# Planned times of DRAM round trips in a two-layer attention encoder

## The chip, the cores and the metric

The kernel runs on one core of a Trainium2 chip. The metric is the device time of one execution, in microseconds; less is better. Each time is the median of the runs made, and one further execution is taken with the hardware profiler, from which all the rows in this document come.

## What is computed

The input is 512 tokens of 1024 numbers, in float32. Two layers follow each other. Each has an RMS norm, one input projection, attention, a gate, an output projection and a residual sum. Layer A, with which the change deals, is dilated window attention with three groups of heads (dilation 1, 4 and 16), 16 heads of 64 in each:

```python
def mixer_a(hn, w_in, w_out, q_gain, k_gain, t5_bias):
    proj = hn @ w_in
    qkv = proj[..., :n_qkv].reshape(b, s, N_DIL_GROUPS, 3, N_HEADS, HEAD_DIM)
    gate = proj[..., n_qkv:]
    for g, (window, dilation) in enumerate(DILATED_PAIRS):
        q = rms_norm(qkv[:, :, g, 0], q_gain[g])
        k = rms_norm(qkv[:, :, g, 1], k_gain[g])
        v = qkv[:, :, g, 2]
        reach = (window // 2) // dilation
        o, lse = dilated_group_attention(q, k, v, t5_bias[g * N_HEADS:(g + 1) * N_HEADS],
                                         dilation, reach)
...
    alpha = jax.nn.softmax(jnp.stack(lses), axis=0)
    y = jnp.sum(alpha[..., None] * jnp.stack(outs), axis=0)
    y = y.reshape(b, s, BRANCH_WIDTH).astype(hn.dtype) * jax.nn.silu(gate)
    return y @ w_out
```

The merge over the three groups by their log denominators equals one softmax over the keys of all three groups together, and the kernel computes it so. Layer B is neighbourhood attention on a grid of 8 x 64 tokens.

## The kernel before

**Numbers and products.** Every float32 weight is split into a high and a low part of TensorE's fast float32 format (`split`, L128 to L139: ScalarE makes the high part `wh`, VectorE or POOL the low part `wl`). A product is then three matmuls: high times high, high times low, low times high (`mm3`, L221). Weights arrive in tiles `wraw` of 512 KB, three of which are in memory; four `wh` and four `wl` are. One split feeds 12 matmuls of 512 columns.

**Layer A by pairs.** The 16 heads are worked in 8 pairs, hc = 0 to 7. For each pair `main_a` projects the keys of two groups together with their values (`rawk`, 96 matmuls), the three groups' queries with the keys of the first (`rawq`, 96 matmuls), then the values of the first group (`v0_a`, 24) and the gate (`gate_a`, 24). The attention of pair hc does not run then. It runs while the next pair is projected: scores in two halves (u = 0 and 1, 96 short matmuls each), softmax, and the weighing of the values (`weigh`, 48 matmuls), which comes a further pair later, ahead of the next pair's scores.

**Trips through DRAM.** Queries and keys lie with tokens in the partitions after the projection, and the scores want heads there. In pairs 0 to 5 (`moved`, L458) the turn is not made on TensorE: VectorE scales the queries and keys by their norms (L313) and turns blocks of 32 x 32 (`turn_raw`, L525 to L530), one DMA writes all of it to DRAM (`qd`, 1536 KB, L654), and four DMAs read it back in the new order (`qt`, L660). Then ScalarE scales the keys (`split_q`, L675: first the keys `k`, L697, then two scalings in `qt`), and the scores can begin. Query buffer, key buffer and the raw queries exist once, so the write must be done before the next pair's keys come out of PSUM. The keys' part of the scaling is delayed (`normed`, L519 to L523), and the turn goes with it.

The first group's values take the same kind of trip (`move_v`, L567 to L589: written to `vd`, read back into `vt`, copied by ScalarE into `v0`), and so do the probabilities P (`turner`, L783: VectorE turns them into `tr`, one DMA writes 1024 KB to `td`, four of 256 KB read them into `pt`). The bias tables `e` are built in DRAM once and loaded for each pair by five DMAs (`bias_a`, L754 to L766).

**What sets the order.** TensorE's order is written by hand. `matmul` adds each matmul's planned time to a clock (`matmul`, L211 to L215), in nanoseconds of a plan and not of the chip. `later_on(delay, job)` emits a job when that clock has moved on by the delay, and the side work (attention) gives out waits such as `"wait", ("rawq", hc), 18000`: go on 18000 after the queries of this pair have been projected. So the constants of the plan say where in TensorE's order a DMA is issued or an operation emitted. The other engines' order comes from a scheduler that simulates the program; DMAs marked `keep_in_program_order` keep their order among themselves on SyncE's queue, which issues all transfers, and so do marked operations on VectorE and ScalarE. Whether an operation is late on the chip is decided by semaphores alone.

The planned times that are touched: the keys' scaling and turn (L520), the values' write, read and copy (L586 to L589), the step from projected queries to the move (L628), the read of the moved queries (L665), the second half's scores of pair 0 (L919), the read of P (L926), and the loading of the tables (L1202 to L1204). `land` (L667) lets the scaling of the moved keys be emitted as soon as the next pair's keys are projected; the first scores come 5200 behind that (L919).

Of the kernel before, what the change touches and what calls it, by code (L numbers as in the profile page):

```python
# [26 lines left out]
NHC = 8  # L27
# [19 lines left out]
def tile_hybrid_encoder(  # L47
# [187 lines left out]
    def later_on(delay, job):  # L235

        timers.append((clock[0] + delay, job))
        timers.sort(key=lambda t: t[0])
# [57 lines left out]
    def head_norm(raw, ss, ns, held, delay=0, quick=False, then=None):  # L296


        rs = wk.tile([P, 32], F32, tag="rs", name="rs")
        rsqrt(nc.vector if ns == 8 or quick else nc.gpsimd, rs[:, : 4 * ns], ss[:, : 4 * ns], 4 * ns, 1.0 / DH)  # L300

        def scale():
            for i in range(4):
                by = rs[:, i * ns : (i + 1) * ns].unsqueeze(2)
                if isinstance(raw, str):
                    f0, f1 = FS[raw]
                    v = by_block[:, :, i, :].rearrange("p (h a f) r -> p f h a r", h=2, f=6)[:, f0:f1]
                    by = rs[:, i * ns : (i + 1) * ns].rearrange("p (f h) -> p f h", h=2)
                    by = by.unsqueeze(3).unsqueeze(4).to_broadcast([P, f1 - f0, 2, 2, 32])
                else:  # L310
                    v = raw[:, i, : ns * 64].rearrange("p (a b) -> p a b", b=64)
                    by = by.to_broadcast([P, ns, 64])
                m = nc.vector.tensor_mul(v, v, by)  # L313
                if held or delay:
                    tc.keep_in_program_order(m)
            if then:
                then()

        if held:
            later.append(scale)  # L320
        elif delay:
            later_on(delay, scale)
        else:
            scale()
# [121 lines left out]
    st = {}  # L446
    pq = wk.tile([P, 4096], F32, tag="pt", name="pt", bufs=1)
# [10 lines left out]
    moved = lambda hc: hc < NHC - 2  # L458
# [58 lines left out]
        normed(raw, ss, ns, key, hc)  # L517

    def normed(raw, ss, ns, key, hc):  # L519
        delay = (31000 if moved(hc) else 9000) if key == "rawk" and 0 < hc < NHC - 1 else 0  # L520
        head_norm(raw, ss, ns, False, delay, then=partial(turn_raw, key) if moved(hc) else None)
        st[key, hc] = raw
        stamp[key, hc] = clock[0]  # L523
# [43 lines left out]
    def move_v(hc, vt):  # L567

        d = dr.tile([4, P, P], F32, name="vd", tag="vd", bufs=2)
        vx = wk.tile([P, 4, 4, 32], F32, tag="vx", name="vx", bufs=1)  # L570
        nc.vector.transpose(vx.rearrange("p b i r -> p i b r"), vt.rearrange("p (i b r) -> p i b r", i=4, b=4))

        def write():
            tc.keep_in_program_order(nc.sync.dma_start(d.rearrange("b p x -> p b x"), vx.rearrange("p b i r -> p b (i r)")))

        def read(b):
            dst = vt[32 * b : 32 * b + 32].rearrange("k (a x) -> k a x", a=4)
            tc.keep_in_program_order(nc.sync.dma_start(dst, d[b].rearrange("(a k) x -> k a x", a=4)))

        def place():  # L580
            src = vt.rearrange("p (a i r) -> p i a r", a=4, i=4)
            dst = v0[hc % 2].rearrange("p i (a r) -> p i a r", a=4)
            tc.keep_in_program_order(nc.scalar.copy(dst, src))
            stamp["v", hc] = 0

        later_on(2500, write)  # L586
        for b in (0, 2, 1, 3):
            later_on(7000, partial(read, b))
        later_on(12500, place)  # L589

    def main_a(hc):
        parts = (
# [32 lines left out]

    def q_a(hc):

        yield "wait", ("rawq", hc), 18000 if moved(hc) else 13000 if hc < NHC - 1 else 23500  # L628
        raw = st.pop(("rawq", hc))
        if moved(hc):  # L630
            move_q(hc)
            return
        qt, k0 = q_tiles(hc)

        tp = transpose4(raw, 0)
        nc.scalar.copy(qt[:, :, 0, :].rearrange("p t (j r) -> p t j r", j=4), to_tjr(tp))
        yield
        tp = transpose4(raw, 3 * P)
        scaled(trj(k0[:, 64:EXT]), to_trj(tp), 0)
        yield  # L640
        for g in range(2):
            tp = transpose4(raw, (g + 1) * P)
            nc.vector.tensor_copy(qt[:, :, 1 + g, :].rearrange("p t (j r) -> p t j r", j=4), to_tjr(tp))
            yield
        stamp["q", hc] = 0

    def move_q(hc):

        d = dr.tile([4, P, 768], F32, name="qd", tag="qd", bufs=2)
        qt, k0 = q_tiles(hc)  # L650
        left = [4]

        def write():
            tc.keep_in_program_order(nc.sync.dma_start(d.rearrange("a p x -> p a x"), by_a))  # L654
            stamp["q", hc] = 0

        def read(a):
            dst = qt[32 * a : 32 * a + 32].rearrange("k t f x -> k t (f x)")
            src = d[a].rearrange("(t k) x -> k t x", t=4)
            tc.keep_in_program_order(nc.sync.dma_start(dst, src))  # L660
            left[0] -= 1

        later_on(600, write)
        for a in (0, 2, 1, 3):
            later_on(5500, partial(read, a))  # L665

        def land():  # L667
            yield "wait", ("rawk", hc + 1), 0
            assert not left[0]
            split_q(qt, k0)  # L670
            yield

        st["land", hc] = land()
# [80 lines left out]
    def bias_a(hc):  # L754
        e0 = wk.tile([P, 2, 256], F32, tag="e0", name="e0")
        e12 = wk.tile([P, 4, 224], F32, tag="e12", name="e12")
        hs = slice(2 * hc, 2 * hc + 2)

        def load(dst, src):
            tc.keep_in_program_order(nc.sync.dma_start(dst, src))  # L760

        load(e0, l0_d[hs].rearrange("h p c -> p h c"))
        for j in range(4):
            dst = e12[32 * j : 32 * j + 32].rearrange("p (h g) c -> p h (g c)", h=2)
            load(dst, l12_d[hs].rearrange("h r c -> r h c"))
        return e0, e12  # L766
# [46 lines left out]
    def attn_a(hc):  # L813
# [99 lines left out]
        if hc < NHC - 1:  # L913
            for u in range(2):
                if moved(hc):
                    if pending and u == 0:
                        pending.pop(0)()
                        yield
                    yield "wait", ("rawk", hc + 1), 5200 if u == 0 else 16800 if hc else 14200  # L919
                else:  # L920
                    yield 6500 if u == 0 else 7000
                turned = turner(512)
                turners.append(turned)
                for hd, t, pr in scores(u):
                    turned.put(pr, 512, 256 * hd + 128 * (t % 2))
                send = partial(turned.send, pq[:, 2048 * u : 2048 * u + 2048], 8500, 1200)  # L926
                later_on(7000 + 2000 * u, send)
                if pending and u == 0:
                    yield 5000
                    pending.pop(0)()  # L930
            pending.append(lambda: put_y(hc, weigh(), True, False))
        else:
            for u in range(2):
                if u == 0:
                    yield "wait", ("gate", hc), 500
                yield 600
                held = scores(u)
                yield 3200
                if pending:
                    yield "wait", ("gate", hc - 1), 16800  # L940
                    pending.pop(0)()
                    yield
                for args in held:
                    turn_p(*args)
                    yield
            yield from v_a(hc)
            stamp["ya", "turned"] = 0
            put_y(hc, weigh(), True, True)
            yield
# [248 lines left out]

    def main():
        for hc in range(NHC):  # L1200
            if hc == 1:
                later_on(20000, lambda: st.__setitem__(("e", 1), bias_a(1)))  # L1202
            elif hc:
                st["e", hc] = bias_a(hc)  # L1204
            yield from main_a(hc)
        yield from out_product("ya", sink_a)
        gap[0] = cycle((500, 500, 800))
        for hc in range(2):
            st["e", hc] = bias_b(hc)
        for kind, i in B_PARTS:  # L1210
            if kind == "qk":
                yield from project_qk(512, 4, "raw", i, ("qk", 2 * i - 1) if i else ("rs", "b"))
            elif kind == "v":
                yield from project_qk(512, 0, "v", i, None)
            else:
                yield from gate_b(i)
        yield from out_product("yb", sink_b, True)
# [153 lines left out]
```

## Time and profile before

| what | us |
|---|---|
| median of 3 runs | 846.79 |
| the runs | 4705.28, 846.79, 845.79 |
| the profiled execution | 845.74 |
| its span, first to last instruction | 844.0 |
| TensorE busy | 831.6 |
| VectorE busy | 516.2 |
| ScalarE busy | 430.4 |
| POOL busy | 282.2 |

The mean granted TensorE clock of the profiled execution is 0.995 of full speed, and the DMA engines moved 154.08 MB at a mean of 183 GB/s. TensorE's busy time counts a matmul from its start to a modelled end, and neighbours overlap, so a busy TensorE says only that no gap is seen, and the sum over groups is more than the span. For the pace one looks at how many matmuls a stretch holds.

In the rows of the timeline the columns are: start in us from the span's start, duration in us, engine, line, operation, what it writes and reads, form, number, and in brackets how long the engine stood idle before it and what ended that. In the rows of waits they are: total us, times, longest us. A window's row has, per engine, busy us and instructions, then the granted clock, the share of the 16 DMA engines, and GB/s. In the chain a row is start, us, what.

### The profile page before, as it was taken

The page shows a single profiled execution, that of the slowest core. Times are in us where ns is not written, and L with a number is a line of the kernel's source. Part 1 is how long each engine was busy: PE and PEld are TensorE (multiplying, and loading weights), DVE is VectorE, ACT ScalarE, POOL GpSimd, SP SyncE. Part 2 cuts the span into 40 slices and gives each one's busy share as a digit, 9 for nine tenths or more (in the row PEclk, how much of TensorE's full clock was granted, in tenths as well). Part 3 has the DMA queues.
Part 4 walks back from the last instruction along what each step waited for, and adds up shares of the span by engine and source line. Part 5 has one row for each costly group of instructions (what it writes and reads, how often), then busy time and mean ns, then how long its engine had stood idle before and what let it go on. Part 6 is the DMA issues. An engine that isn't in the chain of part 4 may idle for free.

```text
span 844.0 us, 15462 instructions
## 1 busy us (share of the span) xinstructions
PE 831.6 (99%) x5616; PEld 669.3 (79%) x5616; DVE 516.2 (61%) x1356; ACT 430.4 (51%) x905; POOL 282.2 (33%) x424
## 2 busy tenths in 40 slices
PE   9999999899999999999999999999999999999998
PEld 7888777688788688788788788888878877777787
DVE  7374575476576467467475665538565678668653
ACT  7443653553653652652662564435366466673551
POOL 2261442442432441441431341112431625225211
PEclk9999999999999999999999999999999999999999
DMA  6487679569569569669668464265226546447323
GB/s 252 131 238 233 179 213 276 169 206 288 164 207 283 134 185 290 181 188 290 182 201 233 139 181 107 67 216 181 100 93 179 167 150 178 136 146 211 103 93 132
DMA packets 73324, 154.08 MB, mean 183 GB/s; under 512 B 6640, under 2 KB 32368, under 8 KB 73248
## 3 DMA queue, kind: packets, MB, share of 16 engines
q1 hardware_dynamic: 73104, 152.83, 60.4%
q8 instruction: 44, 0.72, 0.4%
q10 hardware_dynamic: 144, 0.26, 0.1%
q14 instruction: 32, 0.26, 0.1%
HBM read 117.04 MB, written 39.04 MB: 185 GB/s over the span
## 4 chain that ended last, share of the span: by engine, by line
PE 72%; DMA 13%; DVE 7%; ACT 4%; issue 2%; SPq 1%; POOL 1%; ACTq 0%; DVEq 0%; POOLq 0%
PE acc L215 62%; DMA qt<-qd 5%; PE log L215 4%; DMA qd<-rawq 4%; PE o L215 3%; PE tp L219 2%; DMA e<-l_d 2%; DVE rawq L313 2%; DVE rawq L530 1%; DVE wl L138 1%; ACT p L1140 1%; DMA wraw<-in_w 1%; ACT p L724 1%; ACT qt L697 1%; DMA td<-tr 1%
## 5 line engine op out<-in xcount | busy, mean ns | idle before, releaser
L215 PE MATMUL acc<-wh,hn_h 128*128 128x512 f32 x704 | 281.9, 401 | 1.5 <-ACT hn_h L404 0.6
L132 ACT CAST wh<-wraw 128x512 fp32r<-128x512 f32 (+1 forms) x259 | 157.7, 612 | 235.1 <-PE acc L215 215.1
L215 PE MATMUL acc<-wl,hn_h 128*128 128x512 f32 x704 | 275.0, 391 | 0.2 <-DVE wl L138 0.2
L215 PE MATMUL acc<-wh,hn_l 128*128 128x512 f32 x704 | 274.6, 391 | 0.0
L138 POOL TENSOR_TENSOR wl<-wraw,wh 128x512 fp32r<-128x512 f32 (+1 forms) x104 | 136.4, 1312 | 388.8 <-ACT wh L132 348.3
L138 DVE TENSOR_TENSOR wl<-wraw,wh 128x512 fp32r<-128x512 f32 (+1 forms) x156 | 112.7, 723 | 140.7 <-ACT wh L132 140.2
L215 PEld LDWEIGHTS acc<-wh,hn_h 128*128 128x128 f32 x704 | 132.7, 189 | 38.1 <-issue 6.0
L215 PEld LDWEIGHTS acc<-wh,hn_l 128*128 128x128 f32 x704 | 133.0, 189 | 28.6
L215 PEld LDWEIGHTS acc<-wl,hn_h 128*128 128x128 f32 x704 | 133.2, 189 | 26.2 <-DVE wl L138 0.5
L215 PE MATMUL acc<-y,wh 128*128 128x512 f32 (+1 forms) x272 | 82.4, 387 | 0.0
L215 PE MATMUL acc<-hn_h,wh 128*128 128x512 f32 x192 | 76.1, 396 | 1.2 <-ACT rawk L493 0.6
L215 PE MATMUL acc<-hn_h,wl 128*128 128x512 f32 x192 | 74.8, 390 | 0.0
L215 PE MATMUL acc<-hn_l,wh 128*128 128x512 f32 x192 | 74.8, 389 | 0.0
L724 ACT ACTIVATE p<-p,mn 128x512 f32<-128x512 f32 (+3 forms) x128 | 69.6, 585 | 1.1 <-DVE mn L723 0.7
L290 DVE TENSOR_REDUCE ss<-sq 128x4 f32<-128x256 f32 (+1 forms) x96 | 48.4, 505 | 32.6 <-POOL sq L287 22.5
L878 ACT ACTIVATE p<-p,mn 128x512 f32<-128x512 f32 (+1 forms) x64 | 44.8, 702 | 35.1 <-DVE mn L867 34.7
L794 DVE STREAM_TRANSPOSE tr<-p 128x512 f32<-128x512 f32 (+1 forms) x80 | 53.8, 685 | 12.4 <-ACT p L724 10.0
L313 DVE TENSOR_TENSOR rawq<-rawq,rs 128x256 f32<-128x256 f32 (+1 forms) x96 | 55.0, 632 | 4.1 <-POOL rs L124 3.7
L215 PEld LDWEIGHTS acc<-y,wh 128*128 128x128 f32 x272 | 48.3, 189 | 9.6 <-issue 1.3
L215 PE MATMUL acc<-y,wl 128*128 128x512 f32 (+1 forms) x136 | 51.4, 378 | 0.0
L287 POOL TENSOR_TENSOR sq<-rawq 128x256 f32<-128x256 f32 (+1 forms) x48 | 42.6, 900 | 17.6 <-ACT rawq L493 15.9
L493 ACT ACTIVATE rawq<-acc,rs_n 128x512 f32<-128x512 f32 (+1 forms) x76 | 44.9, 611 | 2.8 <-DMA qd<-rawq 2.5
(123 smaller groups left out, 941.1 us busy)
## 6 DMA issues: line engine op xcount, KB each, us to landing
wraw<-in_w SPq DMA_DIRECT2D x119, 512.0 KB
td<-tr SPq DMA_DIRECT2D x14, 1024.0 KB
pt<-td SPq DMA_DIRECT2D x56, 256.0 KB
qd<-rawq SPq DMA_DIRECT2D x6, 1536.0 KB
qt<-qd SPq DMA_DIRECT2D x24, 384.0 KB
td<-tr SPq DMA_DIRECT2D x6, 896.0 KB
pt<-td SPq DMA_DIRECT2D x24, 224.0 KB
e<-l_d SPq DMA_DIRECT2D x32, 112.0 KB
```

The lines of the kernel that those rows point to most:

```text
L132: nc.scalar.copy(h, raw)
L138: eng.tensor_sub(l, raw, h.bitcast(F32))
L215: nc.tensor.matmul(o, l, r, **kw)
L219: nc.tensor.transpose(o, i, ident)
L287: nc.gpsimd.tensor_mul(sq.rearrange("p (f a r) -> p a f r", a=4, r=32), v, v)
L290: nc.vector.tensor_reduce(ss[:, i * ns : (i + 1) * ns], sq.rearrange("p (a b) -> p a b", b=64), axis=AX.X, op=ALU.add)
L313: m = nc.vector.tensor_mul(v, v, by)
L493: nc.scalar.activation(dst, src, AF.Copy, scale=rs_n[:, i : i + 1])
L530: tc.keep_in_program_order(nc.vector.transpose(x, x))
L724: nc.scalar.activation(pr, pr, AF.Copy, scale=mn[:, 3:4])
L794: nc.vector.transpose(dst, src[:, :n].rearrange("p (i b k) -> p i b k", b=4, k=32))
L878: nc.scalar.activation(row, row, AF.Exp, bias=mn[:, 1:2], scale=-1.0, accum_out=mn[:, 2:3])
```

## The change

Constants of the plan change, and the loading of the tables gets one form for all pairs. No computation, transfer or buffer is added or taken away.

- Pairs 0 to 5: the queries' move begins 8000 behind their projection and no longer 18000; its reads stand 6500 and no longer 5500 behind the move's begin.
- The keys' scaling and turn: 11000 behind their projection (pair 1: 22000) and no longer 31000.
- The values' write, read and copy: 26000, 32000 and 38000 behind their projection (pair 6: 8000, 13000, 18500) and no longer 2500, 7000 and 12500.
- The tables of each pair from 1 on: 26000 after the pair's begin; before, pair 1 had 20000 and the others 0.
- P's second half: its reads begin 6000 behind its write, 500 apart, and no longer 8500 and 1200 apart.
- Pair 0's second half of scores: 12500 and no longer 14200 behind the next pair's keys.

```diff
@@ normed @@
-        delay = (31000 if moved(hc) else 9000) if key == "rawk" and 0 < hc < NHC - 1 else 0
+        delay = ((22000 if hc == 1 else 11000) if moved(hc) else 9000) if key == "rawk" and 0 < hc < NHC - 1 else 0
@@ move_v @@
-        later_on(2500, write)
+        out, back, there = (26000, 32000, 38000) if moved(hc) else (8000, 13000, 18500)
+        later_on(out, write)
         for b in (0, 2, 1, 3):
-            later_on(7000, partial(read, b))
-        later_on(12500, place)
+            later_on(back, partial(read, b))
+        later_on(there, place)
@@ q_a @@
-        yield "wait", ("rawq", hc), 18000 if moved(hc) else 13000 if hc < NHC - 1 else 23500
+        yield "wait", ("rawq", hc), 8000 if moved(hc) else 13000 if hc < NHC - 1 else 23500
@@ move_q @@
         later_on(600, write)
         for a in (0, 2, 1, 3):
-            later_on(5500, partial(read, a))
+            later_on(6500, partial(read, a))
@@ attn_a @@
-                    yield "wait", ("rawk", hc + 1), 5200 if u == 0 else 16800 if hc else 14200
+                    yield "wait", ("rawk", hc + 1), 5200 if u == 0 else 16800 if hc else 12500
...
-                send = partial(turned.send, pq[:, 2048 * u : 2048 * u + 2048], 8500, 1200)
+                send = partial(turned.send, pq[:, 2048 * u : 2048 * u + 2048], *((6000, 500) if u else (8500, 1200)))
@@ main @@
-            if hc == 1:
-                later_on(20000, lambda: st.__setitem__(("e", 1), bias_a(1)))
-            elif hc:
-                st["e", hc] = bias_a(hc)
+            if hc:
+                later_on(26000, lambda hc=hc: st.__setitem__(("e", hc), bias_a(hc)))
```

## The prediction

> **What bounds the kernel now.** I read the page first, then TensorE's waits, its timeline where they fall, the chain, and last the other engines around one stage. The head and part 1 of the page:
>
> ```profile
> span 844.0 us, 15462 instructions
> ...
> PE 831.6 (99%) x5616; PEld 669.3 (79%) x5616; DVE 516.2 (61%) x1356; ACT 430.4 (51%) x905; POOL 282.2 (33%) x424
> ```
>
> TensorE is drawn busy for all but 12.4 us. No edit here removes a matmul, so only idle time and matmuls that run slower than their like can go. TensorE's waits say where the idle time is (total us, times, longest):
>
> ```profile
> PE log L215 <- ACT k L697: 4.5, 4, 2.0
> PE acc L215 <- ACT rawk L493: 1.0, 2, 0.6
> ...
> PE acc L215 <- DVE wl L138: 0.2, 1, 0.2
> ```
>
> The largest is the change's subject: the first scores of a head pair wait for ScalarE's scaling of the moved keys. Here is the start of that score block for pairs 0 to 5, from TensorE's timeline (start, us):
>
> ```profile
> 91.92 0.56 PE L215 MATMUL log<-k,qt 64*32 64x192 f32 x16
> 155.83 0.50 PE L215 MATMUL log<-k,qt 64*32 64x192 f32 x8 [1.98 <-ACT k L697]
> 220.47 0.51 PE L215 MATMUL log<-k,qt 64*32 64x192 f32 x9
> 285.65 0.66 PE L215 MATMUL log<-k,qt 64*32 64x192 f32 x16 [1.81 <-ACT k L697]
> 350.53 0.50 PE L215 MATMUL log<-k,qt 64*32 64x192 f32 x8 [0.25 <-ACT k L697]
> 414.27 0.51 PE L215 MATMUL log<-k,qt 64*32 64x192 f32 x9 [0.50 <-ACT k L697]
> ```
>
> And the projection run behind each block, from the chain in order of time (its start is the block's end):
>
> ```profile
> 93.89 7.07 PE acc L215 x31
> ...
> 159.44 10.16 PE acc L215 x42
> ...
> 223.06 9.74 PE acc L215 x42
> ...
> 289.26 10.13 PE acc L215 x42
> ...
> 353.12 9.77 PE acc L215 x42
> ...
> 416.86 9.74 PE acc L215 x42
> ```
>
> Pair 0, which waits for nothing, takes 93.89 - 91.92 = 1.97 us for its 96 score matmuls. Pairs 1 and 3, after waits near 2 us, take 3.61; pairs 2, 4 and 5 take 2.59. So a late key costs three things: the wait, a longer block (the second and third scaling are late as well), and after a long wait a lower clock, which the stage rows show (us, busy by engine, granted clock, DMA share, GB/s):
>
> ```profile
> 155.80:159.40 3.60, 3.41 (x97) 2.02 (x97) 1.45 (x8) 3.21 (x5) 1.81 (x2) 0.66 0.09 31
> ...
> 192.00:202.00 10.00, 10.00 (x46) 8.29 (x45) 9.51 (x19) 3.22 (x6) 1.33 (x1) 1.00 1.09 261
> 202.00:210.00 8.00, 8.00 (x37) 6.64 (x36) 1.38 (x2) 1.97 (x4) 2.57 (x2) 1.00 1.03 366
> ...
> 219.00:230.00 11.00, 10.82 (x133) 8.16 (x133) 7.14 (x26) 10.22 (x19) 3.65 (x5) 1.00 0.19 70
> ```
>
> What makes the keys late is the trip of queries and keys through DRAM. Pair 1's in the chain, then ScalarE's rows for the scaling in pairs 0, 1 and 3:
>
> ```profile
> 137.04 8.20 DMA qd<-rawq
> 146.61 7.89 DMA qt<-qd
> ```
>
> ```profile
> 90.00 1.24 ACT L697 ACTIVATE k<-qt,gk 128x512 f32<-128x512 f32 x1 [2.60 <-DMA qt<-qd]
> ...
> 154.60 1.17 ACT L697 ACTIVATE k<-qt,gk 128x512 f32<-128x512 f32 x1 [5.75 <-DMA qt<-qd]
> ...
> 284.42 1.17 ACT L697 ACTIVATE k<-qt,gk 128x512 f32<-128x512 f32 x1 [5.58 <-DMA qt<-qd]
> ```
>
> In pair 0 the scaling starts 91.92 - 90.00 = 1.92 us ahead of the scores, and nothing is lost. TensorE alone would have reached pair 1's block at 155.83 - 1.98 = 153.85 and pair 3's at 283.84. So the keys need to be 154.60 - (153.85 - 1.92) = 2.7 us sooner in pair 1, 2.5 us in pair 3, and less in the others. That is the amount that decides.
>
> **The change, part by part.**
>
> *Write sooner (L628: 18000 to 8000), scale of the keys sooner (L520: 31000 to 11000, pair 1 to 22000).* The delays count on the kernel's own clock, which adds up matmul times. Before, write and turn came out together; pair 2's VectorE, POOL and SP rows:
>
> ```profile
> 184.38 2.26 DVE L313 TENSOR_TENSOR rawq<-rawq,rs 128x256 f32<-128x256 f32 x4
> 186.56 0.67 DVE L290 TENSOR_REDUCE ss<-sq 128x8 f32<-128x512 f32 x1
> ...
> 187.82 1.29 DVE L530 STREAM_TRANSPOSE rawq<-rawq 128x512 f32<-128x512 f32 x2
> ...
> 198.78 2.36 DVE L530 STREAM_TRANSPOSE rawq<-rawq 128x1024 f32<-128x1024 f32 x2
> ```
>
> ```profile
> 183.87 1.49 POOL L287 TENSOR_TENSOR sq<-rawq 128x512 f32<-128x512 f32 x1
> ```
>
> ```profile
> 202.18 0.43 SPq L654 DMA_DIRECT2D qd<-rawq  x1
> ...
> 209.90 1.74 SPq L660 DMA_DIRECT2D qt<-qd  x4
> ```
>
> The queries' turn ends at 201.14 and the write goes out at 202.18. An earlier planned write alone therefore buys only about 1 us: the data is not ready. The keys' scale (2.26) and turn (1.29) are in front of it on VectorE. With them gone, the last square sum can follow POOL's square, done at 185.36, and not wait until 186.56 (1.2 us); the keys' turn saves 1.29 more. So the turn ends 2.5 us sooner, and the write goes out at about 198.7, 3.5 us sooner. The bounds are 1.0 (only the gap behind the turn) and 1.04 + 2.26 + 1.29 = 4.6; I take 3.5, which stands on single rows.
>
> The 3.55 us of VectorE work does not vanish. It moves into the first softmax (pair 1's behind the second), in a stretch where VectorE is busy 7.14 of 11 us: 3.9 us are free, so it fits, but just. If that cover is gone, P's turn and its write come up to 3.55 us later; the scores of the second half need only the logits' banks.
>
> *Read back (L665, 5500 to 6500).* From the write's plan the reads stand 5.9 instead of 4.9 us. They wait for the write to land anyway (209.90 is 7.7 us behind 202.18), so this costs nothing while the write takes over 5.9 us. The four reads, in SP's order, still hold up weight loads behind them.
>
> *Values' write, read and copy (L586 to L589) and bias tables (L1202, L1204) later.* Per pair this shifts one write of 256 KB, four reads of 64 KB, five table loads (704 KB, from the tiles' shapes) and one ScalarE copy. Today they run ahead of the query write, at 192 to 202, where the DMA engines are full (share 1.09). Together 1216 KB: at 261 GB/s, 4.8 us of traffic that no longer stands in front of the queries. They move to where the share is 0.19 (219 to 230). Nobody waits for them there: tables are due at the pair's own scores, a pair later, values at its weighing, later still. Pair 6, which moves no queries, has the same in small (5.5 to 6 later). Bounds for the queries' landing: 0, if the weights take the room, to 4.8. I count none of it beside the 3.5; it is my margin over the needed 2.7.
>
> The price is on ScalarE: the copy waits there for the values' reads, and weight splits stand behind it. Before:
>
> ```profile
> 138.45 0.62 ACT L583 COPY v<-vt 128x512 f32<-128x512 f32 x1 [8.83 <-DMA vt<-vd]
> ```
>
> That wait of 8.83 us cost TensorE only the 0.2 us of the wl row above, and the 5.75 us wait at 154.60 cost it no split at all. So a wait below 5.75 us is free and one of 8.83 nearly so. At the new place ScalarE is busy 10.22 of 11 us; a wait there delays softmax too. Bounds: a gain of 0.2 (the wait at 138 goes) to a loss of 8.83 x 6 = 53 us if nothing covered it; I take 0.5 of loss, near the row that cost 0.2.
>
> *P's second half read back sooner (L926: 8500, 1200 to 6000, 500).* Four reads of 256 KB go before the query write instead of between its parts. SP stands still if P's write has not landed:
>
> ```profile
> SPq L807 <- DMA td<-tr: 27.6, 10, 5.8
> ```
>
> One such wait is at most 5.8 us today and starves nothing; I take 0.5 in all, bounds 0 to 5.8. *Pair 0's second scores (L919, 14200 to 12500)* come 1.7 us sooner on the clock. Their matmuls are the same and softmax of the first half covers them: 0; without that cover its P buffer, a single one, would hold VectorE, not TensorE.
>
> **The sum.** Waits: 1.98 + 1.81 + 0.25 + 0.50 = 4.54. A matmul is drawn 0.39 long, but 42 take 9.74 us, 0.23 each, so every one of the four waits is really 0.16 longer: 0.64. Longer blocks: 2 x (3.61 - 1.97) + 3 x (2.59 - 1.97) = 5.14. Slower runs behind pairs 1 and 3: 0.42 + 0.39 = 0.81. One row more goes with the sooner write, which held the evacuation of the next keys:
>
> ```profile
> 146.22 0.50 PE L215 MATMUL acc<-wh,hn_h 128*128 128x512 f32 x1 [0.34 <-ACT rawk L493]
> ```
>
> That is 0.34. All together 11.5 gained, 1.0 given back: 10.5 less. The profiled execution took 845.74 us (span 844.0), so 835.2; the median of the runs, 846.79, stands 1.05 above it, so 836.3.
>
> A page's rule weighs against part of this. The Trainium skill, "TensorE: Matmul & The Clock Gate", Part 1, states that the array's clock falls to half after an idle window of about 3.4 us. By that a 2 us wait should cost no clock, and the slow blocks would have another cause and stay. The trace disagrees: 0.66 granted behind 1.98 us of idling, 1.00 in the row that holds pair 2.
>
> **The rivals.**
> *A, forecast, 836.3:* keys 2.7 us sooner or more in all pairs.
> *B, partly:* VectorE or full DMA engines leave only 1.5 us. Then pairs 2, 4, 5 lose nothing (0.75 + 0.32 + 1.86 gained) and pairs 1 and 3 gain 3.0 of wait but keep 2.59 long blocks (2.04 + 0.81 gained): 8.8 - 1.0, so 839.0; with 0.5 us sooner, some 843. For it: share 1.03 to 1.09 at that place. Against: 1.2 MB less in front.
> *C, slower:* the values' copy stops ScalarE inside softmax. It decides once the wait passes 8.8 us, behind which each further us is TensorE's. With 12 us in each of six pairs, 6 x 3.2 = 19 us lost against 10.5 won: 855. Under 10.5 us each it is no slower than before. For it: this wait reached 8.83; the tables load beside it now. Against: 960 KB of reads at 261 GB/s are 3.8 us, in a stretch with a share of 0.19.
> *D, the clock loss is not the wait's:* the part of pairs 1 and 3 above the other blocks (2 x 1.02 + 0.81 = 2.85) stays: 839.2.
> *E, no effect:* write and reads stay tied to the same landing: 846.8.
>
> **How the numbers follow.** Chances: A 0.66, B 0.14, C 0.08, D 0.06, E 0.06. The time is A's: 836.3. A's own range is 832 to 840: 832 if no price is paid and the 4.8 us also ease later waits, 840 if the prices reach 5. Range for 8 in 10: 831.5 to 844.5, which takes in A, B and D and leaves C and E out. About 2% is what a measurement tells from no change here: that is under 829.9 or over 863.7. Faster by more would take 17 us, beyond the 12.4 us idle plus what slow blocks hold: 0.03. Slower needs C with over 27 us lost: 0.04. Same: 0.93.
>
> **What would show it.** Right: the k row gone from TensorE's waits or under 1 us; blocks of 1.97 us in all six pairs; query writes at least 2.5 us sooner in their stage; no clock under 0.9 between pairs. The keys' scale should lie behind the first softmax. Wrong: ScalarE's values' copy with waits over 8.8 us and TensorE waiting on wh or wl; the wait at log named for logits' banks or P; SP's rows for wraw late behind P's reads.

## The result, and the profile after

The changed kernel takes 830.5 us (median of 4 runs, 830.22 to 832.05). The four runs of the kernel before that belong to this comparison took 4705.28, 846.79, 845.79 and 843.77 us (median 846.29); the ratio leaves the first of them out. The ratio is 0.9827, with a 95% interval of 0.98 to 0.9854: 1.7% faster, some 14.6 us, which is less than the 2% that the prediction takes as the mark of a change. Forecast were 836.3 and a range from 831.5 to 844.5. As measured, the time lies 1.0 us below the range; the ratio applied to the 846.79 from which the prediction counted gives 832.1, which is just inside. The profiled execution took 830.22 us.

The head, TensorE's share and the chain's shares by engine on the page of the changed kernel, and behind them the chain's shares before:

```profile
span 828.4 us, 15450 instructions
...
PE 822.4 (99%) x5616; PEld 667.2 (81%) x5616; DVE 509.5 (62%) x1356; ACT 431.5 (52%) x905; POOL 281.7 (34%) x424
...
PE 94%; ACT 2%; DVE 2%; issue 0%; DMA 0%; DVEq 0%; ACTq 0%
```

```profile
PE 72%; DMA 13%; DVE 7%; ACT 4%; issue 2%; SPq 1%; POOL 1%; ACTq 0%; DVEq 0%; POOLq 0%
```

TensorE's share of the chain that ended last has gone from 72% to 94%, DMA's from 13% to 0%. All of TensorE's waits that the view lists:

```profile
PE busy L379 <- DVE warm L368: 0.9, 1, 0.9
PE acc L215 <- ACT rawk L493: 0.6, 1, 0.6
PE acc L215 <- ACT hn_h L404: 0.6, 1, 0.6
PE acc L215 <- ACT rawq L493: 0.5, 2, 0.3
PE acc L215 <- DVE pt L1039: 0.2, 1, 0.2
```

The row for the scaled keys, 4.5 us before, is gone, and so is the one of `qt` (0.8 us). The first scores of pairs 0 to 5, from TensorE's timeline:

```profile
89.79 0.56 PE L215 MATMUL log<-k,qt 64*32 64x192 f32 x16
...
149.54 0.56 PE L215 MATMUL log<-k,qt 64*32 64x192 f32 x16
...
211.98 0.54 PE L215 MATMUL log<-k,qt 64*32 64x192 f32 x13
...
274.45 0.56 PE L215 MATMUL log<-k,qt 64*32 64x192 f32 x16
...
336.93 0.56 PE L215 MATMUL log<-k,qt 64*32 64x192 f32 x16
...
399.41 0.56 PE L215 MATMUL log<-k,qt 64*32 64x192 f32 x16
```

None has a bracket: no wait. From pair 1 on they stand 62.5 us apart; before it was 63.7 to 65.2. The chain shows the block of pair 1 undivided and the run behind it at the quick pace:

```profile
149.61 1.84 PE log L215 x96
151.46 9.74 PE acc L215 x42
```

Where did the time go? Pair 0 to pair 5 took 414.27 - 91.92 = 322.35 us and takes 399.41 - 89.79 = 309.62: 12.7 less. From there to the end it was 429.7 and is 429.0. The remaining 2.1 us lie ahead of pair 0, where the change touches nothing yet; the last section shows that they are a matter of the start. So the two profiled executions differ by 15.5 us, of which 13.5 can be the change's.

The move of pair 2, from ScalarE's evacuation of the queries over VectorE's turn to SyncE's queue; first before:

```profile
178.78 2.51 ACT L493 ACTIVATE rawq<-acc,rs_n 128x512 f32<-128x512 f32 x4
```

and after:

```profile
170.38 2.51 ACT L493 ACTIVATE rawq<-acc,rs_n 128x512 f32<-128x512 f32 x4
```

```profile
186.51 2.36 DVE L530 STREAM_TRANSPOSE rawq<-rawq 128x1024 f32<-128x1024 f32 x2
```

```profile
186.05 0.35 SPq L184 DMA_DIRECT2D wraw<-in_w  x1
188.90 0.38 SPq L655 DMA_DIRECT2D qd<-rawq  x1
190.18 0.34 SPq L184 DMA_DIRECT2D wraw<-in_w  x1
196.56 1.74 SPq L661 DMA_DIRECT2D qt<-qd  x4
198.41 3.35 SPq L184 DMA_DIRECT2D wraw<-in_w  x2
201.82 0.43 SPq L574 DMA_DIRECT2D vd<-vx  x1
202.30 3.60 SPq L761 DMA_DIRECT2D e<-l_d  x5
```

The write was 23.4 us behind the start of the evacuation (202.18 - 178.78) and is 18.5 us behind it (188.90 - 170.38): 4.9 us sooner. The same subtraction gives 4.8 to 4.9 us in pairs 3 to 5, and 3.2 in pair 1. It leaves when the turn ends, at 188.87. Nothing but weights stands beside the trip; values and tables come behind the reads.

### The profile page after: what moved, and what is told of

Its sections match the earlier page's. It is cut to its first block, busy times and chain, and to the rows that moved or that the text cites. A ratio compares the mean times of both kernels' runs of the same rounds, so it can differ in the third digit from the quotient of the medians.

```text
span 828.4 us, 15450 instructions
## 1 busy us (share of the span) xinstructions
PE 822.4 (99%) x5616; PEld 667.2 (81%) x5616; DVE 509.5 (62%) x1356; ACT 431.5 (52%) x905; POOL 281.7 (34%) x424
## 4 chain that ended last, share of the span: by engine, by line
PE 94%; ACT 2%; DVE 2%; issue 0%; DMA 0%; DVEq 0%; ACTq 0%
PE acc L215 82%; PE o L215 5%; PE log L215 5%; PE tp L219 2%; ACT p L1141 1%; ACT p L725 1%; DVE hn_l L405 1%; DMA x_all<-in_xt 0%; DVE rawq L313 0%; ACT rawq L493 0%; DVE wl L138 0%; DVE pt L1039 0%; ACT wh L132 0%; DVE p L1131 0%; PE pa L215 0%
## 5 line engine op out<-in xcount | busy, mean ns | idle before, releaser
L138 DVE TENSOR_TENSOR wl<-wraw,wh 128x512 fp32r<-128x512 f32 (+1 forms) x156 | 110.5, 709 | 140.9 <-ACT wh L132 140.4
L795 DVE STREAM_TRANSPOSE tr<-p 128x512 f32<-128x512 f32 (+1 forms) x80 | 53.7, 683 | 12.2 <-ACT p L725 10.7
L313 DVE TENSOR_TENSOR rawq<-rawq,rs 128x256 f32<-128x256 f32 (+1 forms) x96 | 50.4, 585 | 4.3 <-POOL rs L124 4.0
L287 POOL TENSOR_TENSOR sq<-rawq 128x256 f32<-128x256 f32 (+1 forms) x48 | 42.2, 891 | 16.3 <-ACT rawq L493 14.5
L289 POOL TENSOR_TENSOR sq<-rawq 128x256 f32<-128x256 f32 (+1 forms) x48 | 34.0, 719 | 34.3 <-ACT rawq L493 27.5
```

The source lines that it names most:

```text
L138: eng.tensor_sub(l, raw, h.bitcast(F32))
L287: nc.gpsimd.tensor_mul(sq.rearrange("p (f a r) -> p a f r", a=4, r=32), v, v)
L289: nc.gpsimd.tensor_mul(sq, v, v)
L795: nc.vector.transpose(dst, src[:, :n].rearrange("p (i b k) -> p i b k", b=4, k=32))
```

## The experiments

My theory on record (M) was that the data's readiness on VectorE and the full DMA engines held the move, and that a write 3.5 us sooner is enough. Its rivals: the planned time alone held it (P), VectorE alone (V), the traffic alone (T), or the values' copy makes it slower (C). After four runs I formed another (S): what counts is what stands behind the write on SyncE's queue.

The lines of the change are put in four groups: A (queries' move at 8000, reads at 6500), B (keys' scale and turn at 11000 and 22000), C (values' trip and tables later) and D (P's second half read sooner, with pair 0's scores at 12500). "Rest" is the span less the start of pair 0's scores, all from the run's profile; it leaves the start out. It comes from one execution of each kernel, so a small difference in it counts only where the waits of that execution show it too. Log, rawk: TensorE's waits for the scaled keys and for the evacuation of raw keys, of which 0.6 lies in layer B in every run. Weights: ScalarE's waits for weight tiles (its rows `wh` waiting for `wraw`).

| kernel | ratio to before (95%) | rest, us | log | rawk | weights |
|---|---|---|---|---|---|
| before | 1 | 752.1 | 4.5 | 1.0 | 2.3 |
| before + A | 1.0253 (1.0218 to 1.0287) | 775.3 | 6.2 | 17.9 | 25.6 |
| before + B | 0.9936 (0.9912 to 0.9959) | 748.9 | 3.9 | 0.6 | 0.5 |
| before + C | 0.9908 (0.9878 to 0.9938) | 744.9 | 2.2 | 0.6 | - |
| before + A, B | 1.0144 (1.0108 to 1.018) | 767.1 | 13.9 | 4.3 | 30.3 |
| the same, copy later | 1.0155 (1.0134 to 1.0177) | 768.5 | 18.8 | 0.6 | 38.5 |
| changed without C | 0.9923 (0.9898 to 0.9948) | 750.0 | - | 8.0 | 11.0 |
| changed without B | 0.9838 (0.9817 to 0.986) | 740.6 | 0.7 | 0.6 | 0.2 |
| changed without D | 0.9857 (0.9835 to 0.9879) | 742.6 | - | 2.7 | 10.8 |
| changed without A | 0.9844 (0.9819 to 0.9869) | 741.2 | 1.0 | 0.6 | 1.1 |
| changed, tables early | 0.9841 (0.9814 to 0.9868) | 742.0 | - | 2.4 | 7.5 |
| changed, values early | 0.9827 (0.9804 to 0.9851) | 738.7 | - | 0.6 | - |
| changed, copy planned sooner | 0.9819 (0.9794 to 0.9844) | 738.6 | - | 0.6 | - |
| changed | 0.9827 (0.98 to 0.9854) | 738.6 | - | 0.6 | - |

Of the kernels that take one edit back, only the one without C lies clear of the changed kernel's interval; for the others the waits and stages of their traces have to show the loss. The profile of the kernel without C is of the slowest of its six runs (843.72 us, median 840.02), so its rest is on the high side.

**A alone.**

```diff
-        yield "wait", ("rawq", hc), 18000 if moved(hc) else 13000 if hc < NHC - 1 else 23500
+        yield "wait", ("rawq", hc), 8000 if moved(hc) else 13000 if hc < NHC - 1 else 23500
...
-            later_on(5500, partial(read, a))
+            later_on(6500, partial(read, a))
```

> The kernel before with one edit alone: the queries' move planned at 8000 (reads at 6500). Theory M (data readiness: VectorE's turn and full DMA engines hold the move, so the plan alone buys about 1 us per pair): keys about 1 us sooner, pairs 2, 4 and 5 stop waiting, pairs 1 and 3 still wait near 1 us; 4 to 6 us faster than before, some 841. Rival P (the planned time alone held it): waits of ScalarE's key scaling at log gone in all pairs, 11.5 us faster, some 835.

It took 867.95 us against 847.71, 2.5% slower. Both theories fell: the sooner plan not only buys little, it costs some 20 us. Most of TensorE's new waits are for raw keys, 17.9 us in all. In pairs 1 to 5 ScalarE stood at the copy of the values, ahead of that evacuation, for 4.3 to 7.2 us; in pair 2:

```profile
214.37 0.62 ACT L583 COPY v<-vt 128x512 f32<-128x512 f32 x1 [6.44 <-DMA vt<-vd]
```

The write of the queries came up on SyncE's queue before its data was ready, and SyncE stood at it for up to 6.5 us, 30.2 us in all; the reads of the values came behind it.

**B alone, C alone.** The diffs are those of `normed`, and of `move_v` and `main`, in the change.

> The kernel before with one edit alone: the keys' scale and turn at 11000 (pair 1 at 22000). Theory M: the turn of the queries ends about 2.5 us sooner, but the write keeps its planned place, so it goes out at most 1 us sooner; 0 to 3 us faster, 843.5 to 846.5. Rival V (VectorE's turn is what bounds the move): waits gone, 11.5 us faster, some 835.

842.28 us, 5.4 less than before: somewhat more than expected, with waits of up to 2.3 us left.

> The kernel before with one edit alone: values' trip and bias tables later. Theory M: the write leaves at the same time, yet its transfer and the reads behind it lose up to 1216 KB of company, 1 to 3 us; also the values' copy no longer holds ScalarE at pair 1 and the evacuation of the next keys isn't held; 4 to 8 us faster, 838 to 842. Rival T (traffic is all of it): waits gone, 11.5 us or more, some 834. Rival C (the values' copy stops ScalarE in softmax): slower than before, with weight splits named in TensorE's waits.

838.84 us, 8.9 less: in the range expected. By the medians C does more than either edit to the move itself, though its interval overlaps that of B. C takes 1216 KB from the road and also takes the copy of the values from in front of the evacuation (ScalarE's waits for it: 25.3 us before, 1.2 here), and this run doesn't part the two.

**A and B, without C and D.**

> The kernel before with two edits: queries' move sooner and keys' scale and turn sooner; values' trip, tables and P as before. Theory M: the write 3.5 us sooner, over the 2.7 us that pair 1 needs, so waits gone in all pairs: 11 to 12.5 us faster, some 834. Rival T (the traffic has to go as well): write sooner but slower, 1 us waits stay in pairs 1 and 3 and values' reads collide with the query write; 840 or more.

859.3 us, 1.4% slower. Rival T's time (840 or more) holds, but not its small waits. This is the case that the prediction's sum would have put at full gain. TensorE's waits:

```profile
PE log L215 <- ACT k L697: 13.9, 5, 4.0
PE acc L215 <- ACT rawk L493: 4.3, 4, 2.9
```

The first row names the same line as before, so one would look for the queries' reads again. But ScalarE's waits of that kernel put them at nearly nothing:

```profile
ACT wh L132 <- DMA wraw<-in_w: 30.3, 5, 7.4
...
ACT v L583 <- DMA vt<-vd: 22.2, 7, 6.3
...
ACT k L697 <- DMA qt<-qd: 0.3, 1, 0.3
```

ScalarE waits for weights, and the keys' scaling stands behind that split on its queue. Its timeline in pair 2:

```profile
220.45 1.14 ACT L132 CAST wh<-wraw 128x512 fp32r<-128x512 f32 x2 [5.84 <-DMA wraw<-in_w]
221.49 1.19 ACT L697 ACTIVATE k<-qt,gk 128x512 f32<-128x512 f32 x1
```

Why the weights are late stands on SyncE's queue, same pair:

```profile
193.15 0.33 SPq L184 DMA_DIRECT2D wraw<-in_w  x1
193.58 0.37 SPq L807 DMA_DIRECT2D pt<-td  x1
196.00 0.38 SPq L654 DMA_DIRECT2D qd<-rawq  x1
196.43 0.50 SPq L807 DMA_DIRECT2D pt<-td  x1
196.97 4.42 SPq L760 DMA_DIRECT2D e<-l_d  x5
201.44 0.43 SPq L807 DMA_DIRECT2D pt<-td  x1
202.68 4.74 SPq L578 DMA_DIRECT2D vt<-vd  x4
207.60 0.30 SPq L807 DMA_DIRECT2D pt<-td  x1
208.21 1.97 SPq L660 DMA_DIRECT2D qt<-qd  x4
210.33 1.31 SPq L184 DMA_DIRECT2D wraw<-in_w  x3
```

Between 193.15 and 210.33 no weight load goes out: 17.2 us, against 8.2 us around the move in the changed kernel (190.18 to 198.41). The sooner write has taken its place ahead of the tables, three reads of P and the values, and they all go out one behind the other, with the weights last. SyncE stood at the write itself for only 2.0 us here; most of the 17.2 us goes to the others. The load that then goes out lands late as well, as the chain shows:

```profile
210.33 10.04 DMA wraw<-in_w
```

How much of the loss is order on the queue and how much is full DMA engines is not parted by these runs. A long stretch without a weight load is not a loss by itself, either: the changed kernel has one of 12.2 us (207.24 to 219.40), in which SyncE waits for a weight tile to come free and TensorE waits for nothing.

**A and B, with ScalarE's copy of the values later.** This takes the copy away from ahead of the evacuation and leaves all transfers where they are.

```diff
-        later_on(12500, place)
+        later_on(38000 if moved(hc) else 12500, place)
```

> The kernel before with queries' move and keys sooner (the pair of edits that took 859 us), and one thing more: ScalarE's copy of the values at 38000, their transfers where they were. Theory S: ScalarE no longer stands at the values' reads ahead of the evacuation, so the waits for rawk (4.3 us there) go; the reads of the moved queries still stand last on the queue, so the waits at log (13.9 us there) stay: 850 to 856. If the copy is all of the loss: 835.

860.21 us, as slow as without it and above the 850 to 856 expected. The waits for rawk went, as expected, but those at log grew from 13.9 to 18.8, and ScalarE's wait for weights from 30.3 to this:

```profile
ACT wh L132 <- DMA wraw<-in_w: 38.5, 5, 8.7
```

So with A and B the copy in front of the evacuation only moved the loss about; what stays in its absence is the late weights. With A alone the copy was not tried at another place.

**The changed kernel, less one edit each.** Each kernel takes back the lines of one letter.

> The changed kernel with values' trip and tables at their old places; everything else as changed. Theory S, formed after the first four runs (the write now takes its place on SyncE's ordered queue ahead of tables and values' reads, these go out while it runs, the reads of the moved queries stand last, and the values' copy holds ScalarE ahead of the evacuation of the next keys): as slow as the kernel with move and keys alone, 850 to 860. My theory M as it was on record (write 3.5 us sooner is enough): 834.

840.02 us, between the two forecasts: D alone, on top of A and B, brings 17 us of the rest, which neither theory had; TensorE now waits for raw keys and no longer for scaled ones. Without C the loss against the changed kernel is 11.4 us of the rest.

> The changed kernel with the keys' scale and turn back at 31000. The queries' turn ends 2.5 to 3.5 us later again. Theory S: with the road clear, pairs 2 to 5 have 3.9 us to spare and wait for nothing, pair 1 has 2.0 and waits up to 1.5: 830.5 to 833. If VectorE's turn is what bounds the move, all pairs wait again: 835 to 841.

833.18 us, just past the end of the range expected, and the one wait (0.7 us) is in pair 3, not in pair 1.

> The changed kernel with P's second half read at 8500, 1200 apart, and pair 0's scores at 14200, as before. Theory S: up to three of P's four reads stand behind the query write on SyncE's queue and run beside it, so the queries land 1 to 3 us later: 831 to 836, with waits in pair 1 first. If P's place is without weight: 830.5.

834.7 us, in the range that theory S expected: 4.0 us of the rest. All of it lies between the scores of pair 0 and those of pair 1, 63.6 us apart here and 59.8 in the changed kernel; from there on both kernels run alike, 62.4 to 62.5 us a pair. And the wait is not for the queries but for raw keys (2.0 us), behind a split that waits for its weights:

```profile
143.31 0.62 ACT L132 CAST wh<-wraw 128x512 fp32r<-128x512 f32 x1 [5.41 <-DMA wraw<-in_w]
```

D has two parts, the reads of P and the second scores of pair 0. Both bear on this one stage, and no run parts them.

> The changed kernel with the queries' move back at 18000 (reads 6500 behind). Theory S: values, tables and P are out of the way and the turn is early, but the write keeps its old planned place, some 9 us later than it now is; waits of the key scaling at log come back small, as in the kernel with the traffic alone (838.8 us): 835 to 840. If the road alone matters and the plan does not: 830.5 to 832.

834.14 us, below the 835 expected at the least: pair 1 alone waits, 1.0 us, and the rest is 2.6 us longer. A is worth little, once the road is clear.

**C in its halves.** One kernel takes back the lines of `main`, one those of `move_v`.

> The changed kernel with the bias tables loaded at the pair's begin, as before; values late. Theory S: five loads of 704 KB stand behind the query write and ahead of its reads on SyncE's queue, 2.5 to 4 us of both; the queries land 3 to 4 us later, pairs 1 and 3 wait 1 to 2 us, or the write is held past the evacuation: 833 to 838.

833.76 us, in the range expected: 3.4 us of the rest. But TensorE waits for raw keys, ahead of the scores of pairs 1 and 5 (1.0 and 0.8 us), and not for scaled ones, and ScalarE again waits for weights (7.5 us).

> The changed kernel with the values' write, read and copy at 2500, 7000 and 12500, as before; tables late. Theory S: only 512 KB, but the ScalarE copy stands ahead of the evacuation of the next keys and the reads of the values stand behind the query write: TensorE waits on rawk as in the kernel without either (8.0 us there), 834 to 840. If the tables are the load and the values are not: 830.5 to 832.

832.24 us: a miss. The rest is the changed kernel's to 0.1 us. The values' reads of 256 KB alone, behind the write, hold nothing up long enough. ScalarE stands at the copy, and TensorE has no row for it:

```profile
ACT v L583 <- DMA vt<-vd: 22.7, 7, 5.0
```

**The copy planned sooner.**

```diff
+        out, back, there = (26000, 32000, 32500) if moved(hc) else (8000, 13000, 18500)
```

> The changed kernel with one constant: the values' copy planned 500 behind their reads, not 6000, so ScalarE meets it in the middle of softmax with the reads still under way. The prediction's price (a wait below 5.75 us on ScalarE is covered by splits made ahead): 830.5 to 831.5 with waits of 3 to 5 us per pair on ScalarE. Rival C (it stops softmax and splits, and TensorE with them): 835 or more, with wl or wh in TensorE's waits.

831.99 us, and no answer: the scheduler placed the copy one or two operations away from where it had been, and ScalarE has no wait for the values' reads. The kernel with values early shows it for another place only: waits of up to 5.0 us on ScalarE, seven of them, ahead of the evacuation of the raw keys, cost TensorE nothing. What such a wait inside softmax costs stays open. No kernel here is clearly faster than the changed one.

## Why the prediction was right and where it was wrong

*The three costs of a late key: right.* All four waits, the long blocks and the slow runs behind pairs 1 and 3 are gone. The prediction's 1.97 us for a block runs from the timeline's start to the next row of the chain; read so, a block is now 1.92 us (151.46 - 149.54), and in the chain alone 1.84, in all pairs from 1 to 5. 11.5 us were counted as gained; 13.5 came behind the start of pair 0's scores. The 1.0 us counted as given back was not: there is no new wait.

*Rival D, the clock loss is not the wait's: wrong.* With the waits gone, no block keeps a low clock.

*The turn 2.5 us, the write 3.5 us sooner: mis-sized.* In pair 2 the turn ends 18.5 us behind the start of the evacuation (188.87 - 170.38) and no longer 22.4 (201.14 - 178.78), 3.9 us sooner, and the write, which now follows at once, 4.9 us sooner. That is past the upper bound of 4.6.

*"An earlier planned write alone therefore buys only about 1 us: the data is not ready": wrong, and the step that failed most.* That the data is not ready was right: SyncE stood at the write for it, 30.2 us in all with A alone. But it was priced as a write that simply waits. On a queue with one order it stands in front of all that is planned behind it. Edit A alone cost 20 us. In the changed kernel SyncE still stands at it, 18.2 us in all and up to 5.9, and nothing comes of it: no tables, values or P are left between the write and its reads. Ahead of the prediction the text says that semaphores alone decide whether an operation is late on the chip; these runs show that its place on the queue decides it too.

*"I count none of it beside the 3.5; it is my margin over the needed 2.7": wrong.* Clearing the road was no margin but what the sooner write needs: A and B without C and D lose 1.4%, with D alone added they gain 0.8%, with both 1.7%. Within C, tables early and values early cost 3.4 and 0.1 us one at a time and 11.4 together, so the edits don't add up. What goes with the loss is ScalarE waiting for weights. It waits 7.5 to 38.5 us in the six kernels that lose by a sooner write (A alone, A and B with the copy early or later, without C, without D, tables early), and not at all in the changed one. The kernel before, B alone and C alone have the old waits for scaled keys instead.

*P's earlier reads, 0.5 us lost: wrong in sign.* In the prediction they were a wait on P's write; in the runs they are reads less beside the query write and ahead of weights. On top of A and B, D brings 17 us, 16 of it between the scores of pairs 1 and 5, where only the reads of P changed. Next to C as well, D is worth 4.0, in the one stage where pair 0's second scores changed too.

*"The four reads, in SP's order, still hold up weight loads behind them": seen, but priced at nothing.* Here lay the slower rival that was missing: not the values' copy in softmax (rival C), but weights behind the move, and with A alone the values' copy at its old place, ahead of the evacuation.

That the number came near all the same is luck in part. The sum credits the gain to the sooner write, and the sooner write without C and D loses; the kernel is fast because the change also held these two, neither of which the sum counts as a gain.

*The keys' scale fits into softmax: right.* The four scalings and the turn of pair 2's keys run while the scores of pair 1 are worked, among the last turns of the first softmax:

```profile
156.81 1.42 DVE L313 TENSOR_TENSOR rawq<-rawq,rs 128x256 f32<-128x256 f32 x4
158.15 1.29 DVE L795 STREAM_TRANSPOSE tr<-p 128x512 f32<-128x512 f32 x2
159.37 1.26 DVE L530 STREAM_TRANSPOSE rawq<-rawq 128x512 f32<-128x512 f32 x2
```

Of the 5.0 us between the sum (835.2 for a profiled execution) and 830.22, about 2.1 are the start's, 2.0 came on top of the 11.5, and 1.0 is the price not paid. Of the 2.0, 0.6 are two waits of TensorE that the sum did not hold, for raw queries (0.38, at 112.32 before) and for a split (0.23, at 140.37); both are gone.

## What to carry to other kernels

Before a transfer is planned sooner, list what is then planned behind it on its queue: a transfer that is not ready, or that goes ahead of many others, delays what stands last there, and if weights are among it the bill comes one engine further on. A wait named for an operation may belong to the one ahead of it on the same engine; look at that engine's own waits before believing the name. And take edits of such a plan back one by one as well as adding them one by one, for the two give different values.

## What the runs showed of the hardware

**The first microseconds.** The executions differ in how fast the first projections run. The row of the stretch from 5 to 10 us, before and then after:

```profile
5.00:10.00 5.00, 4.68 (x11) 3.71 (x12) 4.81 (x8) 4.89 (x9) 0.30 (x1) 1.00 1.02 413
```

```profile
5.00:10.00 5.00, 4.69 (x21) 3.90 (x22) 4.79 (x8) 4.90 (x9) 0.32 (x1) 1.00 1.03 415
```

TensorE began 11 matmuls against 21, with the granted clock recorded as 1.00 in both. Pair 0's scores then start at 91.92 or 89.79. Of the twelve experiments' profiles, some start like the one (values early: 91.82) and some like the other (copy planned sooner: 89.94), though no edit reaches into those first 10 us. A comparison to better than 2 us has to leave the start out. What sets it was not tried.

**A wait and the clock.** The prediction weighed a rule by which a wait of 2 us costs no clock, and let its rows decide against it. The runs show waits with and without a loss. The block of pair 1 in the kernel with B alone, after 2.33 us of waiting, and its stretch:

```profile
155.04 0.66 PE L215 MATMUL log<-k,qt 64*32 64x192 f32 x16 [2.33 <-ACT k L697]
```

```profile
155.00:158.60 3.60, 3.40 (x97) 2.01 (x97) 1.45 (x8) 3.21 (x5) 1.81 (x2) 0.67 0.03 10
```

The block of pair 2 in the kernel with A alone, after 2.64 us:

```profile
226.06 0.51 PE L215 MATMUL log<-k,qt 64*32 64x192 f32 x9 [2.64 <-ACT k L697]
```

```profile
226.00:229.60 3.60, 3.38 (x100) 2.36 (x101) 1.76 (x9) 3.46 (x8) 1.78 (x2) 1.00 0.50 150
```

The longer wait cost no clock, the shorter one did. Pair 2 in the kernel with A and B waited 2.63 us, as long as the last, and had 0.68 granted over the next 3.6 us. So the wait's length alone does not decide at 2 to 3 us. The Trainium skill, "TensorE: Matmul & The Clock Gate", Part 1, describes the window over which activity is watched as one that runs on by itself. That it depends on where a wait falls in such a window would fit these rows, but was not tried.
